# Layer one's MLP with latent and context tokens in one set of seven products, and modulation rows moved to TensorE

## The chip, the cores and the metric

The kernel runs on one core of one Trainium2 chip. The metric is the device time of one execution in microseconds (us). TensorE (PE in the rows; PEld is its weight load) multiplies, VectorE (DVE) and ScalarE (ACT) do elementwise work, GpSimd (POOL) does elementwise work on SBUF, and SyncE (SP) issues nearly all the DMAs. Each engine works through its own queue in order.

## What is computed

A backbone of two layers over 512 latent tokens `x` and 256 context tokens `ctx`, width 1024. Each layer has a mixer (Fourier, attention, convolution), an output projection and an MLP, each with a norm that is modulated by six vectors per token kind:

```python
for l in range(DEPTH):                       # DEPTH = 2
    mx = split(silu(c) @ w_mod[l] + b_mod[l], 6)
    mc = split(silu(c_ctx) @ w_mod[l] + b_mod[l], 6)
    ...                                      # input projection, three mixers, concatenation
    if not last:
        ctx = ctx + mc[2] * (mixed_ctx @ w_o[l])
        hc = rms_norm(ctx, norm2_g[l]) * (1 + mc[4]) + mc[3]
        ctx = ctx + mc[5] * (square(relu(hc @ w_mlp1[l])) @ w_mlp2[l])
    x = x + mx[2] * (mixed_x @ w_o[l])
    hx = rms_norm(x, norm2_g[l]) * (1 + mx[4]) + mx[3]
    x = x + mx[5] * (square(relu(hx @ w_mlp1[l])) @ w_mlp2[l])
return rms_norm(x, final_norm_g)
```

`w_mlp1` is 1024 by 4096. The context runs through the MLP of the first layer only. The first layer is `l == 0` in the code.

## The kernel before

Tensors lie transposed, 128 features on the partitions and the tokens along the columns: 0 to 511 are latent, 512 to 767 context. For precision each fp32 operand is split into a high and a low part, and `mm3` makes one product of three matmuls (high by high, high by low, low by high). ScalarE writes the high part of a weight tile and GpSimd or VectorE the low part (`load_w`, line 152; `block`, line 1055; tables such as `BLOCK` name the engine).

**MLP, up.** The 32 row tiles of the hidden layer are made in 16 pairs. The first three pairs (`first_pairs`) are plain. For the other 13, `pair(p)` uses a scheme with seven products in place of eight on a two by two division: two output tiles by two halves of the tokens, with the inner dimension in two halves of four tiles. The divided operand is the 512 latent tokens, 256 columns a product; each product is 4 inner tiles by 3 matmuls, so 12 matmuls. In the first layer the 256 context columns of each pair are computed beside them without the scheme (`plain`, four calls of 12 matmuls). Weight sums (`sw`, lines 1182 to 1185) and the operand forms (`make_forms`, made once a layer from sums that `sums_of` prepares one inner tile ahead) are the scheme's overhead; the seven results are added on VectorE (line 1210), then `relu2` and `put_hidden` apply the squared ReLU and split it.

**MLP, down.** Between pairs stand two calls of `downs`, each four output tiles of 12 matmuls, half with 512 columns and half with 256. `update` (line 990) adds the result to the residual on VectorE. Three large PSUM tiles go round among the pairs and downs (`psr`); two small ones (`pst`) serve the rest.

**Modulation.** The vectors of 48 groups of 128 features per layer come in three ways. At the start, groups 0 to 15 of layer 0 are computed on TensorE from `wmods` (line 324: `c32` stationary with 32 columns, four inner tiles at a time on four column groups of the array) and turned into columns by `mod_cols`. During the attention, `gate_columns` computes groups 16 to 23 in four pieces, with two stationary columns and 256 moving ones. The others are dot products on VectorE (`mod_group`, line 270: one 128 by 1024 weight tile by DMA, then one reduction of 1024 columns a token kind): groups 24 to 39 during the output projection, three after each output tile; the rest during the MLP of the first layer, four a pair. For the first 16 groups of layer 1, so in the first four pairs that have them, both token kinds are reduced; after that one.

**Order.** The Tile framework orders the instructions of each engine when the kernel is built, by priorities and a model of durations; the queues are fixed then.

## Time and profile before

| what | value |
|---|---|
| time, median of 3 runs | 1632.77 us (1628.58 to 1635.89) |
| the profiled execution: its time, its span | 1634.36 us, 1632.6 us |
| busy share PE, DVE, ACT, POOL | 93%, 76%, 43%, 42% |
| chain that ended last: PE, DVE, DMA, issue | 44%, 30%, 9%, 8% |
| mean granted TensorE clock | 0.982 |
| stage: start and projection of layer 0 | 0 to 110 us |
| stage: mixer of layer 0 | 110 to 352 us |
| stage: output projection and second norm of layer 0 | 352 to 434 us |
| stage: MLP of layer 0 | 434 to 1000 us |
| stage: layer 1, mixer | 1000 to 1210 us |
| stage: layer 1, output projection and MLP | 1210 to 1633 us |

Busy shares are means over stages with different limits, so each edit is read in its own stage. A matmul's end is modelled, so the spacing of the starts, and not the duration of a single record, tells what a matmul costs in a stream. The granted clock 1.00 is 2.4 GHz and a stretch at half of it 1.2 GHz.

### The profile page before, as it was taken

What the parts mean: (1) busy time and instruction counts of PE and PEld (TensorE: products, weight loads), DVE (VectorE), ACT (ScalarE), POOL (GpSimd) and SP (SyncE); (2) the same over time, 40 slices, a digit from 0 to 9 for tenths busy, and PEclk for the clock granted to TensorE, in tenths of its full rate; (3) what the DMA queues carried; (4) which work ended last, traced back from release to release, by engine and by line L of the source; (5) the groups of instructions that cost most, each with busy time, mean ns of one, the idle gap of its engine ahead of it and who ended that gap; (6) DMA issues with size and microseconds to landing.
All of it is one profiled execution on the core that took longest, in us unless ns stands there. A gap on an engine that the chain in (4) does not pass through costs nothing.

```text
span 1632.6 us, 24752 instructions
## 1 busy us (share of the span) xinstructions
PE 1520.0 (93%) x9508; PEld 1329.1 (81%) x9508; DVE 1233.2 (76%) x1984; ACT 698.3 (43%) x1291; POOL 689.1 (42%) x455
## 2 busy tenths in 40 slices
PE   5898999999899999999999999899999979999997
PEld 3598877787788988889999988777878778889897
DVE  3379687779999799987887768978866676566655
ACT  3343577651432333323332244258954434444442
POOL 1415233213135455534444333343325566666671
PEclk9999999999899999999999999999999989999998
DMA  8321102147142333333433332100123122233322
GB/s 282 117 98 57 36 21 86 37 154 250 61 168 67 107 112 117 104 129 125 148 117 105 127 104 99 46 26 8 53 65 117 52 85 91 84 102 104 104 78 65
DMA packets 50567, 159.55 MB, mean 98 GB/s; under 512 B 5745, under 2 KB 13713, under 8 KB 49425
## 3 DMA queue, kind: packets, MB, share of 16 engines
q1 hardware_dynamic: 50016, 152.69, 28.6%
q0 software_dynamic: 432, 5.28, 0.8%
q8 instruction: 75, 1.23, 0.3%
q14 instruction: 44, 0.35, 0.1%
HBM read 155.84 MB, written 2.11 MB: 97 GB/s over the span
## 4 chain that ended last, share of the span: by engine, by line
PE 44%; DVE 30%; DMA 9%; issue 8%; ACT 6%; POOL 3%; SPq 0%; DVEq 0%; ACTq 0%; POOLq 0%
PE ps L156 23%; PE pv L156 10%; DVE mj L270 7%; DMA acc<-in_wmodT 7%; PE tr L156 5%; DVE aw L747 3%; DVE resx L990 2%; PE tr L865 2%; PE po L156 1%; ACT p L849 1%; PE p L156 1%; DVE t L1168 1%; DMA raw<-in_w 1%; DVE resc L990 1%; DVE t L1138 1%
## 5 line engine op out<-in xcount | busy, mean ns | idle before, releaser
L156 PE MATMUL ps<-y,hl 128*128 128x512 f32 (+1 forms) x2004 | 411.2, 358 | 13.0 <-DVE resc L990 4.7
L156 PEld LDWEIGHTS ps<-y,hl 128*128 128x128 f32 x2004 | 328.0, 190 | 74.3 <-DVE resc L990 8.8
L152 POOL TENSOR_TENSOR hl<-raw,hl 128x1024 fp32r<-128x1024 f32 (+2 forms) x92 | 229.8, 2500 | 271.1 <-ACT hl L151 263.1
L156 PE MATMUL pv<-y,hl 128*128 128x512 f32 (+1 forms) x1032 | 212.8, 356 | 5.7 <-POOL hl L152 2.7
L156 PEld LDWEIGHTS pv<-y,hl 128*128 128x128 f32 x1032 | 168.6, 189 | 37.4 <-POOL hl L152 3.2
L151 ACT ACTIVATE hl<-raw 128x1024 fp32r<-128x1024 f32 (+2 forms) x94 | 98.1, 1044 | 226.4 <-PE pv L156 112.0
L1055 POOL TENSOR_TENSOR hs<-raw,hs 128x512 fp32r<-128x512 f32 x95 | 133.2, 1404 | 125.6 <-ACT hs L1054 125.6
L156 PE MATMUL ps<-h,hs 128*128 128x256 f32 (+1 forms) x1080 | 151.2, 292 | 5.3 <-DVE t L1210 3.2
L156 PEld LDWEIGHTS ps<-h,hs 128*128 128x128 f32 x1080 | 140.1, 192 | 11.4 <-issue 3.6
L1054 ACT ACTIVATE hs<-raw 128x512 fp32r<-128x512 f32 x133 | 83.0, 629 | 146.8 <-PE tr L156 30.0
L270 DVE CUSTOM_DVE_ANT_0 mj<-acc,cb,vec 128x1024 bf16<-128x1024 f32 x64 | 103.1, 1611 | 39.7 <-DMA acc<-in_wmodT 39.7
L990 DVE SCALAR_TENSOR_TENSOR resx<-ps,mod,resx 128x512 f32<-128x512 f32 (+1 forms) x134 | 95.7, 719 | 40.2 <-PE ps L156 40.1
L1162 POOL TENSOR_TENSOR y<-t,y 128x256 fp32r<-128x256 f32 (+1 forms) x78 | 73.7, 959 | 120.2 <-DVE t L1168 112.8
L156 PE MATMUL tr<-h,hs 128*128 128x256 f32 x624 | 83.3, 283 | 0.0
L869 DVE TENSOR_TENSOR pT<-tr,pT 128x384 fp32r<-128x384 f32 (+1 forms) x144 | 74.1, 534 | 10.0 <-ACT pT L868 9.4
L868 ACT ACTIVATE pT<-tr 128x384 fp32r<-128x384 f32 (+1 forms) x144 | 65.9, 477 | 32.7 <-PE tr L865 31.7
L156 PE MATMUL pv<-h,hs 128*128 128x256 f32 (+1 forms) x504 | 77.2, 303 | 2.2 <-DVE h L221 2.2
L156 PEld LDWEIGHTS tr<-h,hs 128*128 128x128 f32 x624 | 78.5, 191 | 0.6
L865 PE MATMUL tr<-ident,p 128*128 128x128 f32 x416 | 68.7, 279 | 9.6 <-DVE pT L869 6.8
L156 PEld LDWEIGHTS pv<-h,hs 128*128 128x128 f32 x504 | 69.4, 194 | 5.9 <-DVE h L221 2.6
L156 PE MATMUL po<-pT,v 128*128 128x256 f32 x416 | 72.4, 298 | 1.3 <-DVE t L894 1.1
L1167 ACT ACTIVATE t<-t 128x256 f32<-128x256 f32 (+1 forms) x52 | 32.7, 629 | 93.7 <-DVE t L1210 93.7
(291 smaller groups left out, 2962.0 us busy)
## 6 DMA issues: line engine op xcount, KB each, us to landing
raw<-in_w SPq DMA_DIRECT2D x128, 512.0 KB, 3.7
acc<-in_wmodT SPq DMA_DIRECT2D x48, 512.0 KB, 3.5
raw<-in_wo SPq DMA_DIRECT2D x17, 512.0 KB, 4.3
mq<-in_wmods SPq DMA_DIRECT2D x16, 512.0 KB, 7.9
mw<-in_wmodT SPq DMA_DIRECT2D x16, 512.0 KB, 4.3
ztab<-in_dftx POOLq DMA_DIRECT2D x2, 2064.0 KB, 9.4
gw<-in_wmodg SPq DMA_DIRECT2D x4, 1024.0 KB, 4.9
y<-in_wmodT SPq DMA_DIRECT2D x8, 512.0 KB, 5.4
```

The source lines that it names most:

```text
L151: SC.activation(w[:, 0], raw, AF.Copy)
L152: side[eng].tensor_tensor(w[:, 1], raw, f(w[:, 0]), ALU.subtract)
L156: PE.matmul(o, lhsT=l, rhs=r, start=start, stop=stop)
L270: V.tensor_tensor_reduce(j, w, c[:, v], 1.0, vc("bmod", l, g), ALU.mult, ALU.add, mod[l][v][:, g:g + 1])
L747: V.scalar_tensor_tensor(acw[ct], us[ct][:, i:i + wide], vc("wdw", l, ct * TAPS + i), acw[ct], ALU.mult, ALU.add)
L865: PE.transpose(tr[:, (kt - ka) * P:(kt - ka + 1) * P], ptiles[i][:, kt * P:kt * P + P], ident)
L868: SC.activation(d[:, 0], src, AF.Copy)
L869: V.tensor_tensor(d[:, 1], src, f(d[:, 0]), ALU.subtract)
L990: mark[0] = V.scalar_tensor_tensor(r, pt[:, a - o0:b - o0], mod[l][v][:, gate * 8 + m:gate * 8 + m + 1], r, ALU.mult, ALU.add).ins
L1054: SC.activation(w[:, 0], src, AF.Copy)
L1055: side[eng].tensor_tensor(w[:, 1], src, f(w[:, 0]), ALU.subtract)
L1162: GP.tensor_tensor(ht[:, 1, a:a + n], src, f(ht[:, 0, a:a + n]), ALU.subtract)
```

## The change

- `pair` no longer has the context beside it: the divided operand is all 768 tokens of the first layer (`n2 = nq // 2`), so 384 columns a product, and the four calls of `plain` and the block made for them are gone. The seven results, their sums, `relu2` and the split have 384 and 768 columns. `relu2` runs twice a pair (after products 3 and 4) in both layers; product 4 uses a small PSUM tile (`pst`) in both layers.
- `make_forms` makes its sums itself in one `acc` region and one temporary; `sums_of`, which ran one inner tile ahead, is gone. The fourth form has its own tile (`f4`, pool `fm`, now in both layers).
- `load_mod`, `mod_rows` and `mod_cols` are shared. `gate_columns` takes two pieces of 512 columns (pieces 4 and 5) by the column groups in place of four pieces of 256.
- In the output projection of layer 0, groups 32 to 39 come from TensorE (pieces 8 and 9, after output tiles 1 and 4); groups 24 to 31 stay dot products (2, 2, 1, 1, 1, 1, 0, 0 after the tiles).
- At the start, the low parts of `win0` and the additions of the context's squares go from GpSimd to VectorE.
- `c32` and `sel4` live through the kernel; the scratch of GpSimd's DMAs goes from 4096 to 2048.

```diff
-BLOCK = (dict(zip("x1234567", "PVPVPPVV")), dict(zip("1234567", "PPVPPVP")))
+BLOCK = (dict(zip("1234567", "VPVPPVV")), dict(zip("1234567", "PPVPPVP")))
...
+    def load_mod(q, pl, bufs):
+
+        ws = [pl.tile([P, 2, 512], F32, tag="mq", name=nm("mq"), bufs=bufs) for _ in range(4)]
+        for i, w in enumerate(ws):
+            SY.dma_start(w, A["wmods"][q, :, 2 * i:2 * i + 2])
+        return ws
...
-            wks.append(load_w(A["win0"][k], 896, *((wk, "wk", 6) if k < 6 else ())))
+            wks.append(load_w(A["win0"][k], 896, *((wk, "wk", 6) if k < 6 else ()), eng="V"))
...
         def sq_ctx(kk):
-            sq = acc[:, S:T] if kk == 0 else tmp(C)
-            SC.activation(sq, xt[kk][:, S:T], AF.Square)
-            if kk:
-                GP.tensor_tensor(acc[:, S:T], acc[:, S:T], sq, ALU.add)
+            add_square(acc[:, S:T], xt[kk][:, S:T], kk == 0)
...
         def gate_columns(q):
-
-            w = gp[0].tile([P, KT, 256], F32, tag="gw", name=nm("gw"), bufs=1)
-            SY.dma_start(w, A["wmodg"][q])
-            yield 1
-            pt = pst()
-            for k in range(KT):
-                mm(pt[0:2, 0:256], cpp[:, k], w[:, k], k == 0, k == KT - 1)
...
+            ws = load_mod(q, gp[0], 4)
+            yield 1
+            row = mod_rows(ws, gp[0], 1)
+            yield 1
+            mod_cols(q, row)
             yield 1
...
-        wo_mods = [24, 32, 25, 33, 26, 34, 27, 35, 28, 36, 29, 37, 30, 38, 31, 39]
+
+        wo_mods = {1: 8, 4: 9} if mods else {}
+        wo_dots = (2, 2, 1, 1, 1, 1, 0, 0) if mods else (0,) * KT
+        ready, dots = load_mod(8, mwp, 4) if mods else None, list(range(24, 32))
+        cols_of = []
...
-            if mods:
-                for _ in range(3 if m < NW else 1):
-                    if wo_mods:
-                        w = mwp.tile([P, D], F32, tag="mw", name=nm("mw"), bufs=4)
-                        mod_group(mods, w, 0, wo_mods.pop(0))
+            if cols_of:
+                mod_cols(*cols_of.pop())
+            if m in wo_mods:
+                q = wo_mods[m]
+                cols_of.append((q, mod_rows(ready, mwp, 2)))
+                if q < 9:
+                    ready = load_mod(q + 1, mwp, 4)
+            for _ in range(wo_dots[m]):
+                mod_group(mods, mwp.tile([P, D], F32, tag="mw", name=nm("mw"), bufs=2), 0, dots.pop(0))
...
-        def sums_of(kk):
-
-            ab = (acc[:, 0:2 * n2], acc[:, 2 * n2:4 * n2]) if kk % 2 == 0 else (tmp(2 * n2), tmp(2 * n2))
...
         def make_forms(kk):
...
-            if kk < 3:
-                sums_of(kk + 1)
-            ra, rb = whole_h[kk]
-            t, t3 = tmp(3 * n2), tmp(n2)
-            t1, t2, t4 = (t[:, q * n2:q * n2 + n2] for q in range(3))
+            ra, rb = acc[:, 0:nq], tmp(nq)
+            for x, hk in zip((ra, rb), (h2t[kk], h2t[kk + 4])):
+                (GP if l or kk else V).tensor_tensor(x, f(hk[:, 0]), f(hk[:, 1]), ALU.add)
+            t, t43 = tmp(nq), tmp(nq)
+            t1, t2, t4, t3 = t[:, ua], t[:, ub], t43[:, ua], t43[:, ub]
...
-            for d, x in ((ft[kk][:, :, 0:3 * n2], t), (h2t[kk][:, :, ub], t3)):
+            for d, x in ((ft[kk], t), (f4[kk], t4), (h2t[kk][:, :, ub], t3)):
...
         def pair(p):
...
-            ctx = not last
...
-            oc = [pst()[:, 0:C] for _ in range(2)] if ctx else None
-            if ctx:
-                plain(block(r2[:, 0], BLOCK[l]["x"]), 0, oc[1], True, False)
...
-                    pt[ti] = psr() if ti < 3 or ctx else pst()
+                    pt[ti] = psr() if ti < 3 else pst()
...
-                if ctx and i in (1, 2, 4):
-                    plain(b, int(i > 1), oc[i // 4], i == 1, i != 1)
-                    if i == 2:
-                        put_hidden(ht[0], oc[0], segall[1:])
-            relu2(s, [(slice(0, n2), ht[0], n2), (slice(n2, 3 * n2), ht[1], 0)])
-            if ctx:
-                put_hidden(ht[1], oc[1], segall[1:])
+                if i == 3:
+                    relu2(top, ht[0])
+            relu2(low, ht[1])
...
-    nc = bacc.Bacc("TRN2", target_bir_lowering=False, num_devices=1, dynamic_dma_scratch_size=4096)
+    nc = bacc.Bacc("TRN2", target_bir_lowering=False, num_devices=1, dynamic_dma_scratch_size=2048)
```

## Rows read from the trace of the kernel before

**Rows 1.** The page: busy time of TensorE; the chain that ended last, by engine
```profile
PE 1520.0 (93%) x9508; PEld 1329.1 (81%) x9508; DVE 1233.2 (76%) x1984; ACT 698.3 (43%) x1291; POOL 689.1 (42%) x455
PE 44%; DVE 30%; DMA 9%; issue 8%; ACT 6%; POOL 3%; SPq 0%; DVEq 0%; ACTq 0%; POOLq 0%
```

**Rows 2.** Windows by stage: stretch, length, busy of each engine (instructions), clock, DMA
```profile
236.00:312.00 76.00, 73.06 (x460) 56.49 (x460) 55.96 (x127) 53.94 (x116) 23.27 (x15) 1.00 0.22 72
...
352.00:434.00 82.00, 73.14 (x394) 63.28 (x393) 71.95 (x104) 21.22 (x33) 23.21 (x9) 0.94 0.61 206
...
486.00:523.00 37.00, 35.35 (x198) 29.85 (x197) 36.72 (x61) 11.46 (x17) 18.86 (x10) 1.00 0.18 57
...
554.00:697.00 143.00, 133.66 (x912) 121.68 (x911) 128.83 (x204) 44.94 (x80) 69.60 (x44) 1.00 0.36 118
697.00:964.00 267.00, 260.66 (x1804) 241.28 (x1803) 207.87 (x336) 91.52 (x163) 117.19 (x85) 1.00 0.38 124
...
1296.00:1323.00 27.00, 17.05 (x77) 14.32 (x76) 24.91 (x32) 8.50 (x14) 15.92 (x10) 0.75 0.20 58
```

**Rows 3.** Timeline of TensorE in one pair: start, us, what, count
```profile
837.33 1.60 PE L156 MATMUL tr<-h,hs 128*128 128x256 f32 x12
838.76 1.60 PE L156 MATMUL ps<-y,hs 128*128 128x256 f32 x12
...
850.28 2.25 PE L156 MATMUL ps<-y,hl 128*128 128x512 f32 x12
852.38 2.26 PE L156 MATMUL pv<-y,hl 128*128 128x512 f32 x12
```

**Rows 4.** The chain in order of time, layer 1: start, us, 24 matmuls of 512 columns
```profile
1591.78 5.58 PE ps L156 x24
```

**Rows 5.** A wait of TensorE inside a pair (timeline), and its sum (waits, 520 to 720)
```profile
605.71 1.66 PE L156 MATMUL ps<-y,hs 128*128 128x256 f32 x12 [1.45 <-DVE t L1210]
...
PE ps L156 <- DVE t L1210: 8.1, 5, 2.2
```

**Rows 6.** VectorE in the pairs: one group by form, then two instances on the timeline
```profile
L1210 DVE TENSOR_TENSOR t<-ps,t 128x256 f32<-128x256 f32 x117 | 47.1, 418 | 22.3 <-PE ps L156 20.2
...
612.42 2.04 DVE L1168 SCALAR_TENSOR_TENSOR t<-t,t 128x768 f32<-128x768 f32 x1
...
854.46 0.95 DVE L1168 SCALAR_TENSOR_TENSOR t<-t,t 128x768 f32<-128x768 f32 x1
```

**Rows 7.** The chain in order of time: modulation on TensorE, start then attention
```profile
18.31 2.39 PE tr L324 x16
...
58.85 0.98 PE tr L324 x4
...
67.51 0.80 PE tr L156 x8
...
239.11 3.55 PE tr L156 x16
...
246.45 0.53 PE tr L156 x4
```

**Rows 8.** Output projection of layer 0: a VectorE group, then TensorE's timeline
```profile
L270 DVE CUSTOM_DVE_ANT_0 mj<-mw,cb,vec 128x1024 bf16<-128x1024 f32 x32 | 50.5, 1579 | 4.0 <-DMA mw<-in_wmodT 3.7
...
405.11 0.73 PE L156 MATMUL pv<-y,hl 128*128 128x512 f32 x2 [1.34 <-ACT hl L151]
...
424.17 5.16 PE L156 MATMUL ps<-y,hl 128*128 128x256 f32 x24
...
433.53 6.79 PE L156 MATMUL pv<-h,hl 128*128 128x512 f32 x28 [1.15 <-DVE h L221]
```

**Rows 9.** GpSimd: the forms' sums (groups by form), then its DMAs (the page)
```profile
L1125 POOL TENSOR_TENSOR acc<-h 128x512 f32<-128x512 f32 x6 | 8.3, 1383 | 9.3 <-DVE h L221 5.7 <-DVE t L1138 3.5
...
ztab<-in_dftx POOLq DMA_DIRECT2D x2, 2064.0 KB, 9.4
```

**Rows 10.** Waits of TensorE, 18 to 100: who for whom, total, times, longest
```profile
PE tr L156 <- POOL sq L353: 2.6, 1, 2.6
```

More of the change, by code (lines that the diff above doesn't have):

```diff
@@ L1237, in body @@
         wcfg["raw"] = [(wp, 2)]
-        if last:
-            fm, fm_close = pool("fm")
-            ft += [fm.tile([P, 2, 3 * n2], F32R, name=nm("ft")) for _ in range(4)]
-        else:
-            ft += [unit() for _ in range(4)]
+        fm, fm_close = pool("fm")
+        ft += [fm.tile([P, 2, nq], F32R, name=nm("ft")) if last else unit() for _ in range(4)]
+        f4 += [fm.tile([P, 2, n2], F32R, name=nm("f4")) for _ in range(4)]
         nd = 2 if last else 4
```

131 lines of the change are left out of this document (52 added, 79 removed).

## The prediction

> **What bounds the kernel now.** The page comes first: TensorE is busy 93% of the span, VectorE 76%, and the chain that ended last is 44% TensorE, 30% VectorE and 9% DMA [rows 1]. No single engine is the bound, so each edit is priced in its own stage, and the windows by stage are the second view [rows 2]. In the attention (236 to 312) TensorE is busy 73.06 of 76 us and the others at most 55.96: TensorE leads. In the output projection (352 to 434) TensorE and VectorE are both near their limit, at a mean clock of 0.94. While the forms of layer 0 are made (486 to 523) VectorE is busy 36.72 of 37. The four pair periods with two-sided dot products (554 to 697, "heavy") take 143 us, 35.75 each; the eight after them (697 to 964, "light") take 33.4 each, with TensorE busy 260.66 of 267 and VectorE only 207.87. In the forms stage of layer 1 (1296 to 1323) TensorE does 17.05 of 27 at clock 0.75 and VectorE 24.91. The third view is the timeline of TensorE in one light pair [rows 3], from which a matmul is priced by the spacing of starts.
>
> **Part 1: the products, light pairs.** Twelve matmuls of 256 columns take 838.76 - 837.33 = 1.43 us. A pair has seven products and four plain groups: 11 x 1.43 = 15.73. No record has 384 columns. The bounds are the price at 256, 1.43, and at 512, 5.58 / 2 = 2.79 [rows 4]. The nearest row is a down product, six matmuls of 512 and six of 256, 384 on average: 852.38 - 850.28 = 2.10 [rows 3], and the middle of the two bounds is 2.11. I take 2.10: 7 x 2.10 = 14.70, so -1.03 a pair. If 384 cost as much as 512, a pair would be 3.8 longer.
>
> This pricing can be set against the Trainium skill, TensorE: Matmul & The Clock Gate, Back-to-back issue gap: columns / 2.4 + 2.5 ns. By that rule (an estimate) 132 matmuls at 109 ns become 84 at 162.5 ns, 14.4 to 13.65, -0.76 a pair, so 13 pairs would give -9.9 where the rows give -13.4. The trace has 119 ns at 256, more than the rule, so the rows stand.
>
> The eight light pairs and the first pair of the scheme, which has no dots, are bound by TensorE: 9 x -1.03 = **-9.3**. What is moved off lies beside it: one block fewer a pair on ScalarE and GpSimd costs nothing and gives nothing while TensorE leads. VectorE gets more: 256 columns take 0.418, 768 take 0.95 [rows 6], so 128 more columns are 0.13, and seven sums are +0.9; the ReLU products change from 0.42 + 0.95 + 2 x 0.42 = 2.2 to 2 x 0.95 = 1.9. Net +0.6 on 207.87 / 8 = 26.0 of 33.4: covered. If that cover were gone it would be +0.6 a pair.
>
> **Part 2: heavy pairs.** TensorE's content is 15.73 + 8 x 2.10 = 32.5 of 35.75, so 3.2 idle. VectorE is busy 128.83 / 4 = 32.2, +0.6 after, and waits for its own dot weights in between. TensorE's largest wait is 1.45 us before product 4, on a sum that has yet to empty the PSUM tile (8.1 us in five such waits, [rows 5]); product 4 now takes a small tile, so this wait goes. Late next is the first down product, which takes the tile that the same sums empty, 2.1 us later. Bounds: 0 (VectorE keeps the period) and -4.2 (all idle time and the 1.03). I take -1.0, nearer to 0 because VectorE's 32.8 is above TensorE's new 31.5: 4 x -1.0 = **-4.0**.
>
> **Part 3: gates in the attention.** Four pieces go, each 3.55 + 0.53 on the chain: -16.3. Two come. A piece by column groups took 2.39 in one run of 16 records, but 0.98 for each four when other matmuls stood between, 3.92 a piece; the columns took 0.80 [rows 7]. So +6.4 to +9.4, net -9.9 to -6.9. The DMAs bring the same bytes and were early before. TensorE waits little in this stage, but softmax on ScalarE and VectorE runs beneath the pieces and would be late next, so not all comes through: **-6.0**, bounds -9.9 and -2.
>
> The Trainium skill, TensorEngine Tiling (Array Packing), Key Properties, says that a change of tiling mode drains TensorE, which speaks against this edit. The rows agree that interleaving costs (3.92 against 2.39). By that rule every piece would stand at 3.92, and the four pieces of parts 3 and 4 would cost 6.1 us more than at 2.39; the sums here lie between.
>
> **Part 4: output projection.** VectorE loses 16 dots of 1.579 and their readouts of about 0.1: -26.6 of 71.95. TensorE gains two pieces, +6.4 to +9.4. From 405.11 to the first dense stretch of the MLP at 433.53 [rows 8] there are 28.4 us for 24 matmuls of 512 (5.6) and 48 of 256 (5.7); 17 are waits, the norm's own chain, and a stretch at half clock (24 matmuls in 5.16, against 2.86 at 1.43 per twelve). With VectorE no longer behind I count 11 of the 17 as gone, less 7 of new TensorE work: **-4.0**. Late next is the norm's chain. Bounds: -9 (cheap pieces and all stalls but the chain) and +4 (dear pieces; piece 8 brings 2 MB at the stage's start on SP's queue ahead of the next weights, and TensorE waits behind it).
>
> **Part 5: forms, layer 0.** Per inner tile VectorE has four subtractions 128 columns wider (0.5), one more low part of 384 (0.55) and one 128 wider (0.13): 1.2 x 4 = 4.8, and two wider sums for the first tile, 0.5. This lies on an engine busy 36.72 of 37, so it delays the updates that free PSUM. Product 1 needs no form and gives 2.1 of cover. **+3.5**, bounds 0 and +6.
>
> **Part 6: forms, layer 1.** Widths stay, but sums are no longer one tile ahead: 2 x 1.383 on GpSimd [rows 9] for three tiles, 8.3, if nothing covers them. On the other side, one less overlap of GpSimd with VectorE, whose same instruction takes 0.95 or 2.04 [rows 6]; VectorE is the busy one here. **0**, bounds -6 and +8.
>
> **Part 7: start and small edits.** TensorE waits 2.6 for GpSimd's last squares [rows 10]; on VectorE, mostly idle there, they come sooner, though behind the norm's products. **-1.5**, bounds -4 and +2. Half the scratch for GpSimd's three DMAs (9.4 us to landing, [rows 9]) has no row; I take 0, up to +2, as they are issued long before use. The change of PSUM tile in layer 1 is none, and its earlier ReLU has slack of two down calls: 0.
>
> **Sum.** -9.3 - 4.0 - 6.0 - 4.0 + 3.5 + 0 - 1.5 = -21.3. The profiled execution took 1634.4, so it would be 1613.1; the median lies 1.6 below it, so the forecast is **1611.5**.
>
> **Rivals.** *Heavy pairs become light.* If freeing product 4's tile lets VectorE run without TensorE waiting, each heavy period loses 4.2 and not 1.0: 12.8 more, 1599. For it: the wait's place [rows 5]. Against: VectorE's own 32.8 busy. *VectorE takes what TensorE gives.* Heavy pairs stay, forms cost +6 and +8, the gates give -2, the projection 0: -9.3 - 2 + 6 + 8 - 1.5 = +1.2, so 1634. For it: VectorE is nearly full in the heavy pairs and in both forms stages [rows 2]; against: it loses 26.6 in the projection. *Slower: VectorE sets the period of all pairs.* If the two 768-column ReLU products always meet GpSimd (2.04, not 0.95), VectorE gets 2.2 + 0.9 = 3.1 a pair; 13 x 3.1 = 40, and the other parts give -8: 1665. It decides only when a light period's VectorE time passes TensorE's 31.5, and 26.0 + 3.1 = 29.1 does not. *Not what it says:* 384 columns at the price of 512, 13 x 3.8 - 8 = +41, 1674; the mixed row speaks against it.
>
> **Chances.** The forecast with its neighbourhood (1603 to 1622) 0.55; heavy pairs become light (1590 to 1603) 0.18; VectorE takes it (1622 to 1641) 0.20; slower, both ways, 0.07. About 0.5% (8.2 us) is what a measurement of this kernel can tell from no change: below 1624.6 lie the first two and 0.03 of the third, 0.76; within, 0.17; above 1640.9, 0.07. The range 1594 to 1632 leaves out 0.07 below and 0.12 above.
>
> **What would show it.** Right: products of 12 matmuls at 2.1 us and light periods near 32.4; heavy ones near 34.8 with no wait before product 4; gate pieces at 2.4 to 3.9; VectorE far under its limit in the output projection and no half clock near 424; the forms of layer 0 with more waits of TensorE on line 990's successors. Wrong: light periods that do not shrink, TensorE waiting for piece 8's weights, or a longer forms stage in layer 1.

## The result, and the profile after

The changed kernel takes 1646.1 us (median of 8 runs, 1642.8 to 1649.7) where the kernel before takes 1633.0 in the same series: a ratio of 1.0074 [1.0054, 1.0094], so it is slower by 0.7%. The forecast was 1611.5 with a range of 1594 to 1632: the time lies outside it, on the other side of no change. The profiled execution took 1642.97 us, its span is 1641.2. One execution of a kernel below (mlp_alone) took 2430 us at a mean granted clock of 0.557 and is not in that kernel's median.

First the page (busy time; the chain that ended last by engine), then the windows by stage, as in [rows 1] and [rows 2]:

```profile
PE 1506.2 (92%) x8900; PEld 1312.9 (80%) x8900; DVE 1240.3 (76%) x1949; ACT 685.3 (42%) x1208; POOL 645.1 (39%) x375
...
PE 52%; DVE 26%; DMA 7%; issue 6%; ACT 5%; POOL 4%; SPq 0%; POOLq 0%; DVEq 0%; ACTq 0%
```
```profile
236.00:312.00 76.00, 70.14 (x465) 59.21 (x463) 62.06 (x135) 57.22 (x127) 23.30 (x13) 0.98 0.16 55
342.00:414.00 72.00, 70.07 (x422) 58.39 (x420) 49.97 (x75) 20.85 (x33) 22.74 (x9) 1.00 0.65 223
475.00:522.00 47.00, 32.21 (x152) 27.13 (x151) 43.08 (x56) 10.59 (x15) 20.37 (x9) 0.82 0.15 45
555.00:704.00 149.00, 130.93 (x721) 119.25 (x719) 135.55 (x197) 40.84 (x56) 57.59 (x28) 0.98 0.36 114
704.00:964.00 260.00, 243.01 (x1364) 223.36 (x1363) 200.07 (x309) 79.94 (x110) 99.48 (x51) 0.99 0.37 122
1306.00:1333.00 27.00, 18.05 (x81) 14.39 (x80) 25.58 (x34) 9.03 (x18) 18.28 (x12) 0.83 0.20 55
```

TensorE has 14 us less work (1506.2 against 1520.0), as intended, and yet the span is longer. The second window, the output projection, is better than before: VectorE far under its limit, the clock at 1.00. The third, the forms of layer 0, is the bad one: TensorE 32.21 busy of 47, clock 0.82, VectorE nearly full.

The same landmarks can be found on TensorE's timeline in both kernels, and the time between them tells where the 8.6 us of span came from:

| from one landmark to the next | before | after | difference | forecast |
|---|---|---|---|---|
| start to second output tile of the projection at the start (89.74, 82.36) | 89.7 | 82.4 | -7.4 | -1.5 (part 7) |
| to the second tile of the output projection (355.62, 342.53) | 265.9 | 260.2 | -5.7 | -6.0 (part 3) |
| to the first dense stretch of the MLP (433.53, 414.38) | 77.9 | 71.9 | -6.1 | -4.0 (part 4) |
| to the first pair of the scheme, the forms in it (522.88, 521.75) | 89.4 | 107.4 | +18.0 | +3.5 (part 5) |
| thirteen pairs and downs of layer 0 (960.83, 970.22) | 438.0 | 448.5 | +10.5 | -13.3 (parts 1 and 2) |
| to the end | 671.8 | 671.0 | -0.8 | 0 (part 6) |

So the changed kernel is 19 us ahead when the MLP begins and loses 28.5 in 556 us of it. Most kernels below share the code up to the output projection, and their second tile there starts between 340.2 and 345.8: a difference of 3 us in one profile of that stretch says nothing. Their times from the first landmark to that tile are 258.2 to 263.9, so the -5.7 of the second line is known to some 3 us; the next line is firmer, since that stretch takes 71.1 to 72.0 in all of them.

In a light pair (TensorE's timeline: start, us, count, the wait ahead of it) the products cost what was forecast from [rows 3], and a wait stands in the downs:

```profile
843.71 2.25 PE L160 MATMUL ps<-h,hs 128*128 128x384 f32 x12
845.80 2.25 PE L160 MATMUL ps<-y,hs 128*128 128x384 f32 x12
...
866.55 4.48 PE L160 MATMUL ps<-y,hl 128*128 128x512 f32 x24 [1.62 <-DVE resc L983]
```

845.80 - 843.71 = 2.09 for twelve matmuls of 384 columns. TensorE's own work in a pair is 15 x 2.1 = 31.5 us, and six of the light periods are 33.1 to 34.5 (mean 33.8, where the same six took 33.3 before). The light pair right behind the heavy ones takes 37.2 (before 35.4). Heavy periods are 36.7, 37.7, 36.6 and 38.2, before 35.7 to 36.2.

### The profile page after: what moved, and what is told of

Read it like the earlier page. It is cut to its first block, busy times and chain, and to the rows that moved or that the text cites. A ratio compares the mean times of both kernels' runs of the same rounds, so it can differ in the third digit from the quotient of the medians.

```text
span 1641.2 us, 23189 instructions
## 1 busy us (share of the span) xinstructions
PE 1506.2 (92%) x8900; PEld 1312.9 (80%) x8900; DVE 1240.3 (76%) x1949; ACT 685.3 (42%) x1208; POOL 645.1 (39%) x375
## 3 DMA queue, kind: packets, MB, share of 16 engines
q1 hardware_dynamic: 50592, 152.69, 28.5%
## 4 chain that ended last, share of the span: by engine, by line
PE 52%; DVE 26%; DMA 7%; issue 6%; ACT 5%; POOL 4%; SPq 0%; POOLq 0%; DVEq 0%; ACTq 0%
PE ps L160 29%; PE pv L160 14%; DVE mj L274 4%; PE tr L160 4%; DMA acc<-in_wmodT 3%; DMA raw<-in_w 2%; POOL hl L156 2%; DVE t L1130 2%; DVE hs L1056 2%; DVE aw L751 2%; DVE ac L751 2%; ACT p L842 2%; PE tr L858 2%; PE po L160 1%; DVE t L1149 1%
## 5 line engine op out<-in xcount | busy, mean ns | idle before, releaser
L156 POOL TENSOR_TENSOR hl<-raw,hl 128x1024 fp32r<-128x1024 f32 (+1 forms) x90 | 225.9, 2512 | 295.7 <-ACT hl L155 231.0
L160 PE MATMUL ps<-h,hs 128*128 128x256 f32 (+2 forms) x1080 | 179.5, 318 | 6.2 <-DVE h L225 2.3
L160 PEld LDWEIGHTS ps<-h,hs 128*128 128x128 f32 x1080 | 164.6, 191 | 14.1 <-DVE h L225 2.7
L1056 POOL TENSOR_TENSOR hs<-raw,hs 128x512 fp32r<-128x512 f32 x82 | 121.3, 1481 | 44.6 <-ACT hs L1055 44.5
L1151 POOL TENSOR_TENSOR y<-t,y 128x768 fp32r<-128x768 f32 (+1 forms) x52 | 90.2, 1736 | 91.9 <-DVE t L1149 81.6
L274 DVE CUSTOM_DVE_ANT_0 mj<-acc,cb,vec 128x1024 bf16<-128x1024 f32 x64 | 104.1, 1627 | 28.1 <-DMA acc<-in_wmodT 27.7
L1055 ACT ACTIVATE hs<-sw 128x512 fp32r<-128x512 f32 x78 | 47.8, 630 | 120.3 <-DVE sw L1160 89.7
L179 POOL TENSOR_TENSOR sm<-sm,mhalf 128x2 f32<-128x2 f32 (+2 forms) x16 | 17.8, 1110 | 194.0 <-DVE sm L177 193.9
L1056 POOL TENSOR_TENSOR hs<-sw,hs 128x512 fp32r<-128x512 f32 x26 | 38.0, 1460 | 138.3 <-ACT hs L1055 136.1
L160 PE MATMUL pv<-h,hs 128*128 128x256 f32 (+2 forms) x504 | 82.4, 310 | 0.3
L861 ACT ACTIVATE pT<-tr 128x384 fp32r<-128x384 f32 (+1 forms) x144 | 66.0, 478 | 34.8 <-PE tr L858 33.5
L983 DVE SCALAR_TENSOR_TENSOR resx<-pv,mod,resx 128x512 f32<-128x512 f32 (+1 forms) x70 | 50.4, 720 | 34.4 <-PE pv L160 34.4
```

The costliest lines, as they stand in the source:

```text
L156: side[eng].tensor_tensor(w[:, 1], raw, f(w[:, 0]), ALU.subtract)
L160: PE.matmul(o, lhsT=l, rhs=r, start=start, stop=stop)
L274: V.tensor_tensor_reduce(j, w, c[:, v], 1.0, vc("bmod", l, g), ALU.mult, ALU.add, mod[l][v][:, g:g + 1])
L861: SC.activation(d[:, 0], src, AF.Copy)
L983: mark[0] = V.scalar_tensor_tensor(r, pt[:, a - o0:b - o0], mod[l][v][:, gate * 8 + m:gate * 8 + m + 1], r, ALU.mult, ALU.add).ins
L1055: SC.activation(w[:, 0], src, AF.Copy)
```

## The experiments

The kernel before ran beside every series, and its median lay between 1631.7 and 1636.9. A difference of 2 or 3 us between two kernels of different series is therefore not clear; the ratios, each against the kernel before of the same series, are the better measure. Each stage is read from one profiled execution.

### Which part loses

**old_mlp** keeps every edit but those in the MLP; **mlp_alone** has those of the MLP alone (and the smaller scratch).

```diff
# old_mlp, against the kernel after
-        n2 = nq // 2
+        n2 = S // 2
...
+                if ctx and i in (1, 2, 4):
+                    plain(b, int(i > 1), oc[i // 4], i == 1, i != 1)
# mlp_alone: the reverse, on the kernel before
```

> All edits of the change except those in the MLP: the MLP (products of 256 columns, plain groups, its forms, its block table) is that of the kernel before. Theory: the MLP's edits cost 28 us (forms of layer 0 +18, pairs and downs of layer 0 +10.5, layer 1 -0.8) and the others gain 19 (to the second output tile of the attention -12.9, output projection -6.2), so this kernel takes about 19 us less than the kernel before, some 1614, and its TensorE waits before the first dense MLP product are those of the kernel after. Rival: the gain of the early parts is an offset that the MLP would take back whatever its form, because VectorE bounds the forms and the pairs in both kernels; then this kernel is within 6 us of the kernel before.

> The kernel before with only the MLP's edits (seven products of 384 columns, no plain groups, wider forms). Theory: +18 in the forms of layer 0, +10.5 in its pairs and downs, -0.8 in layer 1, so about 1661 us, 28 above the kernel before. Rival: part of the loss belongs to the earlier arrival at the MLP (weights or dot products of the modulation not yet there); then the MLP alone costs clearly less than 28, say 10 to 18.

old_mlp took 1618.5 us, ratio to the kernel before 0.9894 [0.9862, 0.9926]; mlp_alone 1669.5, ratio 1.0208 [1.0166, 1.0250]. The early edits keep 17 of their 19 us without the new MLP, and the new MLP loses by itself, so the first rival and the second both fall. mlp_alone lost 34 where 28 was expected; its profile shows the forms stage 19.8 longer and pairs and downs 16.6 longer (454.6 us), the rest within what a single profile leaves open. old_mlp is a version that beats both kernels.

### The forms stage

Here TensorE's timeline of the kernel after shows three waits for the update that frees PSUM, each with slow matmuls behind it; then VectorE's timeline in the same stretch, and GpSimd's:

```profile
486.84 6.44 PE L160 MATMUL ps<-y,hl 128*128 128x512 f32 x24 [4.59 <-DVE resc L983]
...
501.83 3.73 PE L160 MATMUL ps<-y,hl 128*128 128x512 f32 x12 [4.34 <-DVE resc L983]
505.39 2.27 PE L160 MATMUL pv<-y,hl 128*128 128x512 f32 x12
507.51 4.38 PE L160 MATMUL ps<-y,hl 128*128 128x512 f32 x24
517.74 4.21 PE L160 MATMUL pv<-y,hl 128*128 128x512 f32 x12 [5.85 <-DVE resc L983]
```
```profile
477.25 2.66 DVE L1130 TENSOR_TENSOR t<-acc 128x384 f32<-128x384 f32 x1
479.83 2.19 DVE L1130 TENSOR_TENSOR t<-t,acc 128x384 f32<-128x384 f32 x1
481.95 0.55 DVE L1130 TENSOR_TENSOR t<-t,t 128x384 f32<-128x384 f32 x1
482.42 0.74 DVE L983 SCALAR_TENSOR_TENSOR resx<-ps,mod,resx 128x512 f32<-128x512 f32 x1
483.08 1.50 DVE L1130 TENSOR_TENSOR t<-t,t 128x384 f32<-128x384 f32 x1
```
```profile
477.10 2.40 POOL L156 TENSOR_TENSOR hl<-raw,hl 128x1024 fp32r<-128x1024 f32 x1 [7.99 <-ACT hl L155]
479.46 2.15 POOL L1125 TENSOR_TENSOR t<-h 128x768 f32<-128x768 f32 x1
482.11 2.06 POOL L1125 TENSOR_TENSOR acc<-h 128x768 f32<-128x768 f32 x1 [0.50 <-DVE t L1130]
```

From TensorE's side the 18 us add up: waits 4.59 + 4.34 + 5.85 = 14.8, where the same stretch before had 1.65; and after each wait the matmuls run at 1.2 GHz for a while, with a mean granted clock of 0.82 in the stage (24 matmuls in 6.44 against 4.38, twelve in 3.73 and 4.21 against 2.27), 5.5 more. That is 13.1 and 5.5, 18.6 in all. From VectorE's side, the first subtraction to the last low part takes 42.6 us (477.25 to 519.88), before 26.3: 5.3 is the wider work, and nine of the twelve subtractions of the first three inner tiles are stretched beyond 0.55, by 14.3 in sum (before about 5, low parts included). A subtraction of 0.55 takes 2.66 because it begins at 477.25 and GpSimd's low part ends at 477.10 + 2.40 = 479.50; the next takes 2.19 because GpSimd's sum ends at 481.61. Each ends 0.4 behind the GpSimd instruction. The update at 482.42, which reads PSUM, runs its plain 0.74 beside the third one.

The Trainium skill, SBUF — State Buffer, SBUF: two separate sides, has this as an exclusive lock: of a VectorE instruction with two SBUF inputs and a GpSimd instruction that reads SBUF, the one that starts first holds the shared port pair for its whole length, and the other one waits. The rows agree: the three stretched subtractions above each end 0.41 behind the GpSimd instruction that was running, so what VectorE loses is the rest of that instruction, not a share of its own.

Two runs take this stage up, one by contention and one by place:

```diff
# sums_v
-                (GP if l or kk else V).tensor_tensor(x, f(hk[:, 0]), f(hk[:, 1]), ALU.add)
+                (GP if l else V).tensor_tensor(x, f(hk[:, 0]), f(hk[:, 1]), ALU.add)
# forms_even
-FORMS = ((0, 1, 1, 2), (1, 3))
+FORMS = ((1, 1, 1, 1), (1, 3))
```

> The kernel after, with the 768-column sums that begin the forms of layer 0 on VectorE for all four inner tiles, not on GpSimd for three of them. Theory of contention: VectorE's subtractions take 2.2 to 2.7 us beside GpSimd's sums and low parts and 0.55 without them; VectorE gets 6 sums of about 0.95 (+5.7) and loses about 14 us of stretching, so the forms stage ends 6 to 9 us earlier than in the kernel after, and the time falls by as much. Rival: the stage is longer because the sums are no longer made one tile ahead and VectorE simply has more to do; then the stage gets longer by the 5.7 us, or does not change.

> The kernel after, with the four inner tiles of layer 0's forms ahead of the first, second, third and fourth call of the downs, one each, and not none, one, one and two. Theory: the forms stage is bound by VectorE's own work, 44.6 us from its first sum to its last low part, of which 14 are stretching beside GpSimd; it starts one call of downs (8.4 us) earlier, where VectorE does dot products that can move, so TensorE's three waits before the first pair shrink by 5 to 8 us. Rival: VectorE is just as full in the stretch before; then the waits move there and the time stays within 2 us.

sums_v took 1647.4, ratio 1.0069 [1.0043, 1.0096]: no gain. Its forms stage is 0.5 us shorter (106.9), not 6 to 9, so it came out as the rival said. GpSimd's low parts of the down weights are still there, and three VectorE instructions still run into them (2.66, 3.16, 3.15). The first of the next two lines would take 0.95 alone; the second is TensorE's last wait of the stage, 5.85 in the kernel after:

```profile
493.21 3.16 DVE L1125 TENSOR_TENSOR t<-h 128x768 f32<-128x768 f32 x1
```
```profile
520.41 4.21 PE L160 MATMUL pv<-y,hl 128*128 128x512 f32 x12 [9.00 <-DVE resc L983]
```

So 7.8 of the stretching went and 5.7 of new work came, where the expectation had counted all 14 as gone. The three waits of TensorE sum to 14.6, against 14.8: the first two are shorter, and the last is longer. That the stretching costs time is thus read from the rows; no run here takes it away without adding work to VectorE. The pairs came out 3.8 longer (452.3), which is not explained. forms_even took 1639.0, ratio 1.0019 [0.9999, 1.0040], 7 below the kernel after, and its forms stage is 7.7 shorter (99.7; the 10.2 that a later expectation names is not what the landmarks give). The same work on VectorE, begun one call of downs earlier, shortens TensorE's waits: VectorE bounds the stage.

**old_even** does the same in the old MLP.

> old_mlp (the old MLP with the change's other edits, 1618.5) with layer 0's forms ahead of the first four calls of the downs, one each. Theory: here the forms stage is 92.1 us from the first dense product to the first pair of the scheme, of which TensorE waits only some 2 to 3 us, so nothing is to be had: within 3 us of old_mlp. Rival: the placing is bad for the old forms too, and 5 us or more come out.

It took 1617.0, ratio 0.9886 [0.9852, 0.9921], within 3 us of old_mlp as expected.

### The light pairs

**blocks_p** puts the low parts of blocks 1 and 7 on GpSimd in all pairs of layer 0, **blocks_mix** in the light ones alone.

```diff
# blocks_p
-BLOCK = (dict(zip("1234567", "VPVPPVV")), dict(zip("1234567", "PPVPPVP")))
+BLOCK = (dict(zip("1234567", "PPVPPVP")), dict(zip("1234567", "PPVPPVP")))
# blocks_mix, on the kernel after
-                product(i, block(src[i], BLOCK[l][str(i)]), o[i])
+                product(i, block(src[i], BLOCK[l or int(p > 7)][str(i)]), o[i])
```

> The kernel after, with the low parts of weight blocks 1 and 7 of layer 0's pairs on GpSimd and not on VectorE. Theory of bunching: VectorE has its work at the end of a pair and is 4 to 6 us late for the sums of the downs, where TensorE waits 1.6 to 1.9 a period; without two blocks (one of them 2.15 us) it is in time, the light period falls from 33.8 to about 32 and the layer gains 10 to 20 us. Rival: GpSimd is slow on these blocks and TensorE then waits for weights of product 1 and product 7, or the stretching on VectorE takes the gain; then no change or slower.

> The kernel after, with the low parts of blocks 1 and 7 on GpSimd in the eight light pairs of layer 0 alone; the heavy pairs keep them on VectorE. With them on GpSimd throughout (blocks_p), the light pairs fell from 33.8 to 32.9 and the heavy ones rose from 37.3 to 39.3. Theory: VectorE is late at the end of a light pair, and GpSimd's stretching of dot products is what hurts the heavy ones; then this kernel keeps 37.3 and 32.9, 7 us less than the kernel after. Rival: the rise of the heavy pairs had another cause than the blocks (the placing of the dot products), and the gain of the light ones is lost again here: within 2 us of the kernel after.

blocks_p took 1641.2, ratio 1.0031 [1.0010, 1.0053], 5 us below the kernel after where 10 to 20 were expected: light pairs 33.0 in the mean, but heavy ones 38.8 to 39.8. blocks_mix took 1637.8, ratio 1.0011 [0.9993, 1.0029], 8 below, with light pairs of 32.7 to 33.3 and heavy ones of 37.0 to 39.4. That bears out bunching in the light pairs, only in part: 31.5 was not reached.

**nodots_after** and **nodots_old_mlp** leave out the dot products of layer 1's modulation and their loads.

```diff
+    for v in range(2):
+        V.memset(mod[1][v], 0.0)
...
             ll, g = todo.pop(0)
+            if ll:
+                return
```

> The kernel after without the dot products and weight loads of layer 1's modulation, which stand in the pairs and downs of layer 0 (left out: layer 1's modulation, which is set to zero). Theory: the seven products of 384 save TensorE the 1.03 us a pair that was forecast, but VectorE, whose queue holds the dot products between the products' sums and the updates that free PSUM, is late; without them every pair from the fourth on takes 31.5 to 32.2 us, TensorE's waits for updates go, and pairs and downs of layer 0 shrink from 448.5 to about 412; the kernel takes about 1610. The forms stage stays at 107. Rival: the pairs are held by latency (weight loads, blocks, three PSUM tiles), not by VectorE's load; then light pairs stay above 33 and the kernel gains only what the heavy pairs lose, 37.3 to 33.8 in four of them, 14 us.

> The kernel with the change's other edits and the old MLP (old_mlp, 1618.5), without the dot products and weight loads of layer 1's modulation (left out: layer 1's modulation, which is set to zero). Its TensorE content is 32.5 us a pair. Theory: pairs fall to about 32.7, so from 439 to about 424 for the stage and to some 1604 in all; beside the kernel after without the dot products the pairs are then 0.8 to 1.0 us a pair slower, some 12 us, and the forms stage 15 us shorter, so that the two kernels come within 6 us of each other. Rival: here too the pairs hardly fall; then the dot products cost the old form nothing, and the difference of the two without them stays near the 28 us it is with them.

nodots_after took 1620.8 (0.9910 [0.9881, 0.9939]), nodots_old_mlp 1593.8 (0.9742 [0.9708, 0.9775]). Without dot products the old form runs at 32.6 us a pair in all twelve, TensorE's own work and not a wait. The new form does not reach its 31.5: ten of twelve periods are 33.1 to 33.5. So the theory that VectorE's load held the light pairs fell, and the two kernels are 27 us apart where 6 were expected. The rival's first half is right, they are held by something else, though the kernel gained 25 us and not 14; VectorE's timeline in nodots_after shows it, then TensorE's, its waits for updates (526 to 948; total, times, longest), and the window of this period (length; busy of TensorE, its weight load, VectorE, ScalarE, GpSimd):

```profile
841.14 0.96 DVE L1153 SCALAR_TENSOR_TENSOR t<-t,t 128x768 f32<-128x768 f32 x1 [0.91 <-ACT t L1152]
842.02 0.55 DVE L1188 TENSOR_TENSOR t<-tr,t 128x384 f32<-128x384 f32 x1
842.54 2.10 DVE L1060 TENSOR_TENSOR hs<-raw,hs 128x512 fp32r<-128x512 f32 x1
844.57 0.95 DVE L1153 SCALAR_TENSOR_TENSOR t<-t,t 128x768 f32<-128x768 f32 x1
845.44 0.74 DVE L985 SCALAR_TENSOR_TENSOR resx<-ps,mod,resx 128x512 f32<-128x512 f32 x1
846.10 0.47 DVE L985 SCALAR_TENSOR_TENSOR resc<-ps,mod,resc 128x256 f32<-128x256 f32 x1
```
```profile
846.62 4.48 PE L162 MATMUL ps<-y,hl 128*128 128x512 f32 x24 [1.47 <-DVE resc L985]
```
```profile
PE ps L162 <- DVE resc L985: 11.0, 7, 1.7
PE pv L162 <- DVE resc L985: 5.7, 4, 1.5
```
```profile
826.15:859.37 33.22, 31.75 (x182) 29.28 (x182) 21.79 (x33) 10.21 (x14) 12.70 (x8) 1.00 0.19 64
```

The first down product is complete when the second begins, near 840.8. Its update stands in VectorE's queue behind the first ReLU product (with 0.91 of waiting for ScalarE), the last sum, block 7's low part (2.10 beside GpSimd, 0.68 alone) and the second ReLU product, and starts 4.6 late. The first three down products fill the three large PSUM tiles, and the fourth waits. VectorE is busy only 21.79 of the 33.22 us and idles elsewhere in the period: it is the order of its queue, not its load.

**nodots_late** and **late_relu** take two of these out of the way. The order is written with a scheduling hint: the second ReLU product behind the second update of the next downs.

```diff
-BLOCK = (dict(zip("1234567", "VPVPPVV")), dict(zip("1234567", "PPVPPVP")))
+BLOCK = (dict(zip("1234567", "VPVPPVP")), dict(zip("1234567", "PPVPPVP")))
...
-            relu2(low, ht[1])
+            late.append((low, ht[1]))
+            if l or p == NPAIR - 1:
+                relu2(*late.pop())
...
                 update(o, j * n + mi, 5, whole, None)
+                if late and j * n + mi == 1:
+                    with tc.issue_after(mark[0]):
+                        relu2(*late.pop())
```

> As the kernel after without the dot products of layer 1's modulation (left out: that modulation, set to zero), and in layer 0 the ReLU product of a pair's second row tile stands on VectorE behind the second update of the downs that follow, and block 7's low part is on GpSimd. In that kernel a pair takes 33.2 us, TensorE waits 1.47 for an update, and on VectorE the block's low part (2.10) and this ReLU product (0.95) stand between the end of the first down product and its update. Theory of queue order: with both out of the way the updates are in time and the periods fall to 31.5, the twelve of them by 1.7 each, so some 20 us to 1600. Rival: another step of the loop is late (weight load, the ReLU product of the first row tile); then the periods stay above 32.8.

> The kernel after with the same two edits (the second ReLU product behind the second update of the downs, block 7's low part on GpSimd in layer 0) and all dot products. Theory of queue order: light pairs fall from 33.8 to about 32 (8 x -1.8), heavy ones by about 1 (4 x -1.0), so some 18 us less than the kernel after, about 1628. Rival: with the dot products VectorE's load leaves no room, the waits come back behind the dot products, and the gain is below 6 us.

nodots_late took 1603.6 (0.9790 [0.9760, 0.9820]), late_relu 1629.4 (0.9957 [0.9935, 0.9979]): 17 us below the kernels they were made from (19 by the ratios), both near what the theory of queue order gave. VectorE's timeline in nodots_late at the same place, and the one wait of TensorE from 524 to 920 (total, times, longest), at the last pair:

```profile
822.98 0.96 DVE L1153 SCALAR_TENSOR_TENSOR t<-t,t 128x768 f32<-128x768 f32 x1 [0.91 <-ACT t L1152]
823.85 0.55 DVE L1188 TENSOR_TENSOR t<-tr,t 128x384 f32<-128x384 f32 x1
824.32 0.74 DVE L985 SCALAR_TENSOR_TENSOR resx<-ps,mod,resx 128x512 f32<-128x512 f32 x1
824.98 0.47 DVE L985 SCALAR_TENSOR_TENSOR resc<-ps,mod,resc 128x256 f32<-128x256 f32 x1
```
```profile
PE ps L162 <- POOL y L1155: 2.1, 1, 2.1
```

All twelve periods are 31.5: beside the 32.6 of the old form, the 1.03 a pair of part 1 is there in full, 1.1, once these two no longer stand ahead of the updates. In late_relu, dot products and all, light pairs are 31.5 to 32.4. The two edits were not run apart; blocks_mix, with block 7 and block 1 moved alone, stops at 32.7. Even so nodots_late is 10 us behind nodots_old_mlp: its pairs and downs take 403.5 against 417.0, but its forms stage takes 109.2 against 92.2.

### The heavy pairs

late_relu's heavy pairs are still 35.3 to 38.0. **late_even** adds the even forms; **spread**, **spread_late** and **spread_old** change the order of the modulation's groups in the kernels after, late_even and old_even, so that each pair has 5.3 reductions.

```diff
-        todo = [(0, g) for g in range(40, 48)] + [(1, g) for g in range(48)] if mods else []
+        todo = [(0, g) for g in range(40, 48)] + [(1, g) for i in range(16) for g in (i, 16 + 2 * i, 17 + 2 * i)] if mods else []
```

> late_relu with layer 0's forms ahead of the first four calls of the downs, one each. The even placing alone gave 10.2 us in the forms stage and 7 in all. Theory: both gains add, so about 1620, below the kernel before. Rival: the dot products that the earlier forms push back meet the late ReLU products in the heavy pairs, and not more than 5 us come on top of late_relu.

> The kernel after with the 48 groups of layer 1's modulation in another order alone: each two-sided group is followed by two one-sided ones, so that all twelve pairs from the fifth on hold 5.3 reductions in place of 8 in four and 4 in eight. Theory: a heavy pair is long because its 8 reductions stand in VectorE's queue ahead of sums and updates, and a light one because of the queue order (second ReLU product, block 7) that this kernel keeps; so heavy pairs fall by about 3 and light ones rise by 0.3: 4 x -3 + 8 x 0.3, about -10, some 1636. Rival: each reduction costs the same wherever it stands (448.5 - 425.4 = 23 us for 64, 0.36 each); then nothing changes.

> late_even (second ReLU product behind the second update, block 7 on GpSimd, forms one a call) with the modulation's groups in the spread order. Theory of queue order: with VectorE's work spread evenly and the updates ahead of it, seven products of 384 columns are held by TensorE's 31.5 us: the four heavy pairs fall from 38.2 to about 33 and the light ones rise from 31.9 to 32.3, so 18 us less than late_even, about 1604, 14 below old_mlp. Rival: two-sided reductions hold the pairs where they stand; then less than 6 us, and the old MLP stays ahead.

> old_even (the old MLP with the change's other edits, forms one a call) with the modulation's groups in the spread order. Its heavy pairs took 36 and its light ones 32.9, at 32.6 of TensorE's own. Theory of queue order: all twelve come to about 33.3, 4 x -2.7 + 8 x 0.4, so -8: about 1609, behind spread_late by the 1.03 us a pair that the products of 384 save, less the longer forms. Rival: nothing changes, as each reduction costs the same wherever it stands.

late_even took 1622.2 (0.9914 [0.9881, 0.9947]), as its theory had it: faster than the kernel before. Its heavy pairs are 37.8 to 39.3, longer than late_relu's, so what its rival feared is there in part. spread took 1634.5 (0.9993 [0.9975, 1.0012]), 12 below the kernel after where 10 was expected. Its profiled execution is one of its longer ones, 1639.8, and 3.2 below that of the kernel after; there the pairs are 5.1 shorter (443.3) and the forms stage is 2.3 longer. spread_late took 1633.0 (0.9973 [0.9950, 0.9997]), 11 above late_even and 29 above what was expected: its pairs lie at 33.1 to 36.5, none at 31.5 but the first. spread_old took 1623.1 (0.9903 [0.9879, 0.9926]), no better than old_even, where 8 less was expected. So an even load helps the kernel after and not the other two. The waits of VectorE (530 to 960; total, times, longest), of late_even and then of spread_late, show one thing that grew:

```profile
DVE mj L274 <- DMA acc<-in_wmodT: 25.9, 25, 1.9
```
```profile
DVE mj L274 <- DMA acc<-in_wmodT: 44.4, 24, 3.0
```

All these dot products share one landing tile; VectorE stands at a reduction until its weights have landed, with sums and updates queued behind. It is not the whole account: in spread this wait grew too, from 27.7 to 37.5, and the pairs became shorter, and in spread_late the 64 reductions themselves take 116.0 in place of 105.2. Why the spread order helps one kernel and hurts the other stays open. **late_noload** takes the wait away and keeps the arithmetic; **old_dots2** gives the old form, where there is room, a second tile.

```diff
# late_noload, on late_even
-        SY.dma_start(w, A["wmodT"][l, g])
+        if load:
+            SY.dma_start(w, A["wmodT"][l, g])
...
-                mod_group(mods, w, ll, g, 2 if ll == 0 or g < 16 else 1)
+                mod_group(mods, w, ll, g, 2 if ll == 0 or g < 16 else 1, ll == 0 or g == 0)
# old_dots2, on old_even
-                            more_mods(acc)
+                            land.append(land.pop(0))
+                            more_mods(land[0])
```

> late_even with all its dot products, but the weight tile of layer 1's modulation is loaded once and not for each group (left out: the right values of layer 1's modulation). VectorE's arithmetic is the same; what goes is its wait for the tile, 25.9 us in 25 places in late_even and 44.4 in spread_late, with sums and updates queued behind. Theory of the wait: the heavy pairs are long, and the spread kernels uneven, because VectorE stands in order at a dot product whose weights have not landed; then the heavy pairs fall from 38.2 to 34 or less, and the kernel from 1622 to about 1604. Rival, load: 8 reductions a pair, many stretched beside GpSimd, fill VectorE; then heavy pairs stay at 37 or more, and the gain is below 5 us.

> old_even (the old MLP, the change's other edits, forms one a call, about 1617) with two landing tiles in turn for the weights of the dot products in place of one. Theory of the wait: a tile's load no longer begins after the reductions of the group before, so VectorE does not stand waiting for it; heavy pairs fall from 36 to 33.5 and light ones to 32.7, 12 us in all, to about 1605. Rival, load: VectorE's own work holds the heavy pairs; then within 4 us of old_even.

late_noload took 1610.9 (0.9859 [0.9839, 0.9878]), 11 below late_even where 18 was expected: the heavy pairs fell from 38.2 to 33.8 (33.6, 33.6, 33.6, 34.3), light ones rose to 32.7. The reductions themselves (group by form: count, busy, mean ns, idle before) in about four heavy periods of the kernel before, of the kernel after, of late_even and of late_noload:

```profile
L270 DVE CUSTOM_DVE_ANT_0 mj<-acc,cb,vec 128x1024 bf16<-128x1024 f32 x31 | 48.8, 1575 | 13.5 <-DMA acc<-in_wmodT 13.5
```
```profile
L274 DVE CUSTOM_DVE_ANT_0 mj<-acc,cb,vec 128x1024 bf16<-128x1024 f32 x31 | 58.4, 1882 | 5.8 <-DMA acc<-in_wmodT 5.4
```
```profile
L274 DVE CUSTOM_DVE_ANT_0 mj<-acc,cb,vec 128x1024 bf16<-128x1024 f32 x31 | 61.4, 1982 | 4.3 <-DMA acc<-in_wmodT 4.2
```
```profile
L275 DVE CUSTOM_DVE_ANT_0 mj<-acc,cb,vec 128x1024 bf16<-128x1024 f32 x32 | 50.2, 1569 | 0.0
```

The wait alone is small in the heavy pairs (4.2 us in four). What differs is where the reductions stand: one of 1.27 alone takes 1.98 in the mean in late_even, since it meets GpSimd; without loads 19 of 31 that begin in the four periods take the plain 1.27 to 1.30, against 8 of 31, and all take 50.2 us in place of 61.4. With windows of late_even and late_noload over four heavy periods the account closes:

```profile
547.00:700.00 153.00, 135.35 (x722) 122.97 (x721) 141.84 (x192) 40.81 (x56) 62.15 (x32) 0.94 0.37 113
```
```profile
546.00:681.00 135.00, 128.24 (x721) 116.55 (x720) 130.07 (x195) 38.67 (x56) 64.45 (x32) 1.00 0.20 63
```

18 us shorter: 11.8 less VectorE time, all but 0.6 of it the reductions, and 6.2 less idle VectorE. So both theories were partly wrong. Load it is, VectorE is busy 130 of 135 us even then, but the load is made in good part by when each reduction runs, and taking the weight loads away changed that. It is a matter of place and not of total; in the light pairs (700 to 945) of late_even and of late_noload it goes the other way:

```profile
L274 DVE CUSTOM_DVE_ANT_0 mj<-acc,cb,vec 128x1024 bf16<-128x1024 f32 x31 | 41.1, 1324 | 21.9 <-DMA acc<-in_wmodT 21.8
```
```profile
L275 DVE CUSTOM_DVE_ANT_0 mj<-acc,cb,vec 128x1024 bf16<-128x1024 f32 x28 | 49.0, 1752 | 0.0
```

All 64 reductions take 105.2 in late_even and 106.2 in late_noload. Whether a second landing tile would do for the new form what the missing loads did was not run. old_dots2 took 1616.0 (0.9885 [0.9860, 0.9910]), within 4 us of old_even, with heavy pairs of 35.5 to 36.4: the wait for the tile is gone from them, and they are no shorter. That is the rival's forecast, but VectorE idles 12 of 144 us in those pairs and TensorE waits 8.2 in four places for an update, so full load is not shown to hold the old form either.

### The start

**win_p** puts the low parts of the input weights on GpSimd again.

```diff
-            wks.append(load_w(A["win0"][k], 896, *((wk, "wk", 6) if k < 6 else ()), eng="V"))
+            wks.append(load_w(A["win0"][k], 896, *((wk, "wk", 6) if k < 6 else ())))
```

> The kernel after with the low parts of layer 0's input weights on GpSimd again (the squares of the context stay on VectorE). The start came 7.4 us earlier in the kernel after (second output tile of the projection at 82.36, before 89.74). Theory: GpSimd's low parts, 2.1 to 2.6 us each, stretch VectorE's work and hold back what TensorE needs, so most of the gain goes with them: 4 to 6 us longer than the kernel after, some 1651. Rival: the squares alone made it, GpSimd's three late sums having stood ahead of the norm; then within 1.5 us of the kernel after.

It took 1647.8, ratio 1.0097 [1.0069, 1.0124], against 1.0074 [1.0054, 1.0094] for the kernel after: some 4 us more by the ratios, but the intervals overlap, and the landmarks say it better. The one at 82.36 comes at 87.75, so 5.4 of the 7.4 are the low parts. The kernels below that share this start have it between 81.2 and 84.0, so the 5.4 is clear of the scatter and the 2.0 left for the squares is not. The windows from 73 to 106 of the kernel before, of the kernel after and of win_p:

```profile
73.00:106.00 33.00, 29.21 (x177) 25.71 (x177) 17.03 (x34) 11.09 (x24) 4.68 (x6) 0.90 0.16 54
```
```profile
73.00:106.00 33.00, 32.54 (x236) 30.25 (x235) 23.38 (x40) 11.43 (x26) 5.05 (x4) 1.00 0.13 45
```
```profile
73.00:106.00 33.00, 30.90 (x198) 27.24 (x198) 20.75 (x41) 12.20 (x26) 2.08 (x3) 0.95 0.17 55
```

A late step shows twice here: TensorE is busy less (29.21, 32.54 and 30.90 of 33), and the granted clock is lower where it waited (0.90, 1.00 and 0.95).

## Why the prediction was wrong, step by step

**Part 1, light pairs (-9.3; these nine pairs measured +4.8): the price was right, the cover was not.** 2.10 was taken for a product and 2.09 measured, 174 ns a matmul; the 384 columns at the price of 512 is out. By the formula of the Trainium skill, TensorE: Matmul & The Clock Gate, Back-to-back issue gap, which the page gives for a single isolated matmul, 384 columns would take 162.5 ns (an estimate). The rows lie above it here too, as they did at 256. The two rows behind VectorE's +0.6 came out (seven sums cost 0.92 more, the ReLU products 0.3 less), but its busy time did not grow: 26.15 us in each of the six light pairs, where the same six had 26.4 before. The step that failed is "Net +0.6 on 26.0 of 33.4: covered". A busy share says nothing of where in the queue the work stands. Both ReLU products of 768 columns, with a pass of ScalarE between, and block 7's low part now meet at the pair's end, ahead of the updates that free PSUM: in nodots_after the first update starts 4.6 late, and TensorE waits some 1.5 a pair for it. nodots_late shows the -1.03 when that is put right.

**Part 2, heavy pairs (-4.0, measured +5.7 in four).** The wait of [rows 5] did go, and late next was indeed the first down product: it waits 1.73 for a sum, and a later one 2.42 for an update:

```profile
608.49 2.38 PE L160 MATMUL ps<-y,hl 128*128 128x512 f32 x12 [1.73 <-DVE t L1184]
...
617.50 3.90 PE L160 MATMUL ps<-y,hl 128*128 128x512 f32 x12 [2.42 <-DVE resc L983]
```

But the forecast let VectorE grow by 0.6 from 32.2; it grew to 135.55 / 4 = 33.9, because the reductions went from 48.8 to 58.4 us. The bound of 0 on the bad side was wrong: a reduction took from 1.27 to 2.89 in these periods, and its place was free to change. What holds the heavy pairs was only in part settled (late_noload).

**Part 3, gates (-6.0): right**, -5.7 from the landmarks, known to some 3 us; no run has this edit alone. **Part 4, projection (-4.0): right in kind, -6.1.** The half clock near 424 went, as said (the last line below; the same 24 matmuls took 5.16 before), and the pieces cost less than both prices taken:

```profile
351.05 1.93 PE L288 MATMUL tr<-mq,c 128*32 128x512 f32 x16
...
361.44 0.95 PE L160 MATMUL tr<-sel,mr 128*128 128x2 f32 x8
...
407.08 3.12 PE L160 MATMUL ps<-y,hl 128*128 128x256 f32 x24
```

1.93 + 0.95 = 2.9 a piece in all four, where 3.2 to 4.7 was counted: no piece was cut up by other matmuls.

**Part 5, forms of layer 0 (+3.5, bound +6, measured +18.0): mis-sized, and the largest single term.** The 5.3 of wider work was right by the rows. Left out were the sums that now run beside the subtractions of their own tile (9 us of stretching, priced by no row although [rows 6] has 2.04 for 0.95) and the clock that TensorE loses after each wait (5.5). The stretching is read from the rows and not shown by a run of its own; that VectorE bounds the stage is shown by forms_even. The pair's first product gave no cover, since TensorE waited before it, in the downs.

**Part 6, layer 1 (0): right in sum**, -0.8; no run tells its two opposite terms apart. **Part 7, start (-1.5, bound -4, measured -7.4): mis-sized**; the low parts were not priced, only the squares. The halved scratch (0) was not run apart.

**The rivals.** The nearest was the one held for 0.07 with the other, VectorE setting the period of all pairs; its condition, that VectorE's time must pass TensorE's 31.5, was the error, since 26.15 was enough. The early parts came 7.7 better than forecast and the MLP 38 worse.

## What to carry to other kernels

Before calling an addition on a second engine covered, list what stands in that engine's queue between a result and the instruction that frees its PSUM tile, with the waits for other engines in that list; count that against the number of free tiles, not the busy share against the period. Price a VectorE instruction with two SBUF inputs at its own time plus the rest of whatever GpSimd may be running, and look at what a moved step newly stands beside. Where an edit has parts in different stages, measure them apart: here the early edits with the old MLP take 1617 to 1619, 1% under the kernel before, and the new MLP takes 1622 with a queue order of its own.

## What was not expected of the hardware

- A VectorE instruction with two SBUF inputs waits beside GpSimd to the end of GpSimd's instruction: 0.55 becomes 2.66, 0.95 becomes 3.16, 1.27 becomes 2.65, while updates that read PSUM keep 0.74.
- After a wait of 4.59 in the forms stage the granted clock fell so that 24 matmuls took 6.44 in place of 4.38. After waits of 1.47 and 1.62 in the pairs 24 took 4.48, so those cost hardly more than themselves; after the one of 2.42 at 617.50 twelve took 3.90 in place of 2.27.
- Pieces by column groups, 16 records in a row, took 1.92 to 1.93, against 2.39 in the start before [rows 7] and 2.74 in the start after; why the start is slower is not shown.
